# Forward substitution of the RWKV mixer's diagonal blocks: from GpSimd to VectorE, in three stretches for eight

## The chip, the cores and the metric

The kernel runs on one core of one Trainium2 chip. The time is device microseconds of one execution; it is timed several times and the median counts. The engines go by the profile's names: PE is TensorE's matmul, PEld its weight load, DVE is VectorE, ACT is ScalarE, POOL is GpSimd, SP is the engine that only issues DMAs. Each engine works through its own queue in order; engines wait for each other by semaphores.

## The reference

One step of a two-layer network, D = 2048, on 288 tokens: 256 of a prompt and 32 of a running stream. Layer 0 mixes with an mLSTM and an RG-LRU, layer 1 with RWKV-7 (32 heads of 64 channels); each layer ends with a squared-ReLU MLP. All is fp32. The change lies in layer 1's token mixer, whose core is a recurrence over tokens:

```python
def step(S, inp):
    r_t, k_t, v_t, kk_t, a_t, w_t = inp
    sa = jnp.einsum('bhvk,bhk->bhv', S, -kk_t)
    S = S * w_t[:, :, None, :] + sa[..., None] * (kk_t * a_t)[:, :, None, :] + v_t[..., None] * k_t[:, :, None, :]
    return S, jnp.einsum('bhvk,bhk->bhv', S, r_t)
```

The kernel does it in chunks of 64 tokens. Within a chunk the updates form a unit triangular system, so that each head and chunk needs T = (I - M)^-1 of a strictly triangular 64 x 64 matrix M. There are 32 heads and 5 chunks, 160 such matrices.

## The kernel before

All matmuls are three passes in two float32r parts: a weight slab of 128 x 1024 is loaded (`raw`), its high part `whi` is copied by ACT and its low part `wlo` is subtracted on DVE (line 132, shown as L78 since a helper issues it).

The stage that matters comes after the projections of k. Heads go in 16 pairs. Three streams are traced side by side at line 1216, and the framework's list scheduler puts their instructions in order on each engine, by priority and by its own estimate of when each can start; the order is then fixed in the program.

- `front(p)` (line 981), two pairs at a time: elementwise work on DVE and ACT for one pair (`tw`, `L`, `kkn`, `big`), ten small matmuls that give M of the pair (line 1027, shown in traces as `pm<-big`), then `nm`, M masked, on DVE (line 1036). `nm` goes to DRAM as `n` (line 1042) and `big` as well (line 1044).
- `inverse16(q)` (line 1049), two at a time, q = 0 to 7: for the pairs 2q and 2q + 1. The 80 diagonal blocks of 16 x 16 (2 pairs, 2 heads, 5 chunks, 4 blocks each) come back from DRAM as `nb` [80, 16, 16] (line 1055, a DMA issued by POOL), `tb` is loaded with unit matrices, and 15 steps of forward substitution run on the 80 partitions at once, each a product `tmp<-nb,tb` and a sum `tb<-tb,tmp` of (15 - s)(s + 1) elements, 15 to 64. This is called a solve below; it is 30 operations, and 240 in the eight. It runs on `IE`, which is POOL. After each odd s the generator yields, so it is traced in eight stretches. The result goes to DRAM as `t` (line 1070, two DMAs).
- `inverse(p, nm)` (line 1082), run for the two pairs when the solve is through: `tq` comes back from DRAM (line 1089, issued by POOL), DVE transposes it to `xq` (line 1108), PE multiplies it with `nm` (line 1109, in traces `pm<-tq,nm`), DVE masks the product to `zz`, PE multiplies (`pm<-zz,xq`), DVE adds to `t32` and transposes it to `x32`; from there the off-diagonal block (`pm<-t,nm`, `pm<-z,x`) and T of the pair, to DRAM at line 1148.
- Beside them the dense products of v and r (`ps<-hC,whi` and the like), 931 matmuls of 288 columns in this stage.

`nm` has 7 buffers, so that front p waits for the inverse of pair p - 7; `nb` has one buffer, so that the next one is loaded when the solve has read the last one; `whi` and `wlo` have three. The stage that follows, `wkv`, has an order written out by hand; its first matmul transposes `bk` (`pm<-cst,bk`, line 1283). It starts when the last inverse is through.

Of the kernel before, what the change touches and what calls it, by code (L numbers as in the profile page):

```python
# [11 lines left out]
OP = mybir.AluOpType  # L12
# [4 lines left out]
N = NP + NS  # L17
KT = D // 128
KS = 8
# [17 lines left out]
# columns of the constants  # L37
# [4 lines left out]
def stream_step(ctx: ExitStack, tc: tile.TileContext, I, O):  # L42
# [92 lines left out]
    def slab_in(src, pool_, tag, w):  # L135
        """slab, its parts in tiles of another pool"""
        raw = wp.tile([128, KS, 128], F32, name="raw", bufs=3)
        SP.dma_start(raw, src)
        hi, lo = ([pool_.tile([128, N], F32R, name=f"{c}s", tag=tag, bufs=32)[:, :256].rearrange("p (a b) -> p a b", a=2)
                   for _ in range(KS // 2)] for c in "hl")  # L140
        w += [(hi[k // 2][:, k % 2], lo[k // 2][:, k % 2]) for k in range(KS)]
        for j in range(KS // 2):
            r = raw[:, 2 * j:2 * j + 2]
            copy(hi[j], r)
            yield
            tt(lo[j], r, hi[j].bitcast(F32), OP.subtract)
# [25 lines left out]
    def dense(srcs, xs, m=128):  # L172
        """psum[m, N] = W.T @ x; srcs: one DRAM slab for every KS tiles of xs"""
        ps = psum.tile([128, 512], F32, name="ps", bufs=NPS)
        n = len(xs)
        for s, src in enumerate(srcs):
            kt = min(KS, n - s * KS)
            wh, wl = slab(src, kt, m)
            for k in range(kt):
                g = s * KS + k  # L180
                mm3(ps[:m, :N], (wh[:, k, :], wl[:, k, :]), xs[g], g == 0, g == n - 1)
        return ps[:m, :N]

    def load2(pl, src, bufs):
        """slab of two tiles, in space of its own"""
        raw = pl.tile([128, 2, 128], F32, name="raw2", bufs=bufs)
        SP.dma_start(raw, src)
        return raw
# [19 lines left out]
    def dense_g(srcs, xs, m=128, step=4, rest=1):  # L208
        """dense, which lets others on after every step tiles; two at a time"""
        yield from hold()  # L210
        ps = psum.tile([128, 512], F32, name="ps", bufs=NPS)
        n = len(xs)
        for s, src in enumerate(srcs):
            kt = min(KS, n - s * KS)
            wh, wl = slab(src, kt, m)
            for k in range(kt):
                g = s * KS + k
                mm3(ps[:m, :N], (wh[:, k, :], wl[:, k, :]), xs[g], g == 0, g == n - 1)
                if g % step == step - 1:
                    for _ in range(rest):  # L220
                        yield
        free()
        return ps[:m, :N]
# [11 lines left out]
    def run(*streams, n=0):  # L235
        """traces generators side by side, of each stream as many as its width, until all from stream n on are through"""
        rnd[0] = 0
        while any(gens or on for gens, _, on in streams[n:]):
            rnd[0] += 1
            for gens, width, on in streams:  # L240
                while gens and len(on) < width:
                    on.append(gens.pop(0))
                step(on)
# [12 lines left out]
    # squares are taken of d = y - c, where c is the mean of the first CF tiles:  # L256
    # (mean - c)^2 <= (KT / CF - 1) var, so that var = E d^2 - (E d)^2 loses next to nothing
    CF = 2

    class Norm:  # L260
# [7 lines left out]
        def before(self, x, scale=None):  # L268
            """what the next tile is added to, times scale: takes c off already"""
            if len(self.ys) >= CF:  # L270
                if scale:
                    stt(x, x, scale, self.cen, OP.mult, OP.subtract)
                else:
                    tt(x, x, self.cen, OP.subtract)
            elif scale:
                ts(x, x, scale, None, OP.mult, OP.bypass)

        def add(self, y):
            """takes the next tile; the last is left out of the sums"""
            k = len(self.ys)  # L280
            self.ys.append(y)
            if k == 1:
                gadd(self.acc, self.ys[0], y)
            elif 1 < k < CF:
                gadd(self.acc, self.acc, y)
            if k == CF - 1:
                pc = pm()[:, :N]
                mm(pc, ones, self.acc)
                act(self.cen, pc, AF.Copy, scale=1.0 / (128 * CF))
                for j in range(CF):  # L290
                    tt(self.ys[j], self.ys[j], self.cen, OP.subtract)
                    self.sums(j)
            elif k >= CF:
                self.sums(k)
# [14 lines left out]
        def finish(self, gname, bname, out, mid=lambda k: [], subv=(0,)):  # L309
# [22 lines left out]
            with tc.manual_schedule():  # L332
# [5 lines left out]
                # two steps of third order: r <- r (15 - 10 h + 3 h^2) / 8, h = x r^2  # L338
# [34 lines left out]
    class Lead:  # L373
        """the first four matrices after a norm, of two slabs each, three of them at a time"""
# [5 lines left out]
        def ahead(self):  # L380
            """the first slabs"""
            for src, w in list(zip(self.srcs, self.w))[:3]:
                run1(slab_in(src[0], *self.pt, w))

        def mid(self, k):
            """the second slabs, in the course of the norm"""
            i = MID.get(k)
            if i is None:
                return []
            return [slab_in(self.srcs[i][1], *self.pt, self.w[i]) if i == 2 else self.second(i)]  # L390
# [27 lines left out]
    # =================================================================  # L418
    # layer 0
    # =================================================================  # L420
# [6 lines left out]
    # gates of the mLSTM, with the first queries  # L427
# [35 lines left out]
    def log1p(out, z, t1, t2):  # L463
        """log(1 + z) for 0 <= z <= 1, by s = z / (2 + z)"""
# [40 lines left out]
    # RG-LRU constants  # L505
# [57 lines left out]
    def mlstm(h, t):  # L563
# [13 lines left out]
        # attention of the tokens  # L577
# [14 lines left out]
        # numerators and the denominator, which every partition gets  # L592
# [20 lines left out]
        # new state  # L613
# [14 lines left out]
        # norm over the head  # L628
# [41 lines left out]
    def lru(g, xp, yg, wg):  # L670
# [19 lines left out]
        # sqrt(1 - a^2) = (1 + a) sqrt(tanh(u / 2)), a = exp(-u)  # L690
# [12 lines left out]
        # tanh gelu  # L703
# [44 lines left out]
    def mlp(layer, xs, first):  # L748
        """X <- alpha X + mlp(X), xs: X in parts"""
# [23 lines left out]
    # the blocks of 16, zero beside the diagonal  # L773
# [9 lines left out]
    def shift(xx, x, k):  # L783
        """the token before, less the token"""
# [12 lines left out]
    # mixes: 0 r, 1 w, 2 k, 3 v, 4 a, 5 g  # L797
# [29 lines left out]
    # =================================================================  # L827
    # layer 1
    # =================================================================
    # per-channel constants  # L830
# [8 lines left out]
    def head_sums(st, x):  # L839
        """st[96, 6] = the sums over the channels of the two heads, for 3 blocks of tokens"""  # L840
        for j in range(3):
            mm(st[:, 2 * j:2 * j + 2], x[:, 96 * j:96 * j + 96], blk[:, 0:128:64])
# [92 lines left out]
    def over_head(pl, y, bufs):  # L935
        """psum[128, N] = y[96, 6] over the channels of a head"""
# [16 lines left out]
    def prod(out, l, x, start=True, stop=True):  # L953
        """out = l^T x for the two heads, which lie on the halves of the partitions"""
# [18 lines left out]
    IE = G  # L973
# [7 lines left out]
    def front(p):  # L981
# [19 lines left out]
        # decays, summed within the chunks  # L1001
# [22 lines left out]
        # strictly lower M = A B^T, as [s, t]  # L1024
# [24 lines left out]
    def inverse16(q):  # L1049
        """(I - M)^-1 of the 16 x 16 blocks on the diagonal, two pairs of heads"""  # L1050
# [7 lines left out]
        for s in range(15):  # L1058
# [4 lines left out]
               tb[:, s, :n].unsqueeze(1).to_broadcast([80, w, n]), OP.mult, eng=IE)  # L1063
            tt(tb[:, s + 1:, :n], tb[:, s + 1:, :n], tv, OP.add, eng=IE)
            if s % 2:
                yield
# [15 lines left out]
    def inverse(p, nm):  # L1082
        """T = (I - M)^-1 for each chunk of the two heads, to DRAM"""
# [67 lines left out]
    def feed():  # L1151
        """the products beside the heads, tile by tile: queries, then the first half of the output projection with what
        it is added to, to DRAM; slabs are loaded two ahead and split one ahead"""
# [77 lines left out]
    def beside(gens, width, gap, other, rate, size):  # L1231
        """traces gens, as many as width at a time and gap rounds apart, with rate steps of other for each of a round"""
# [22 lines left out]
    def wkv(p):  # L1255
# [21 lines left out]
        def tok(x, out):  # L1277
            """[channel, token] to [token, channel], by head and chunk"""
# [38 lines left out]
        # head h of a stack: its own rows, and the other half of the partitions  # L1317
# [19 lines left out]
        # y, which the chunks add up to; the first one of the prompt clears the bank  # L1337
# [5 lines left out]
        def chunk(c, st, pu, pS, out=None):  # L1343
            """adds to y; the state, at sv[., c], to the next place, or to out"""
# [51 lines left out]
        # norm over the head, bonus, gate  # L1396
# [85 lines left out]
def _pack(np, a):  # L1482
    """lays the inputs out for the chip"""
# [5 lines left out]
    def slabs(w, m=128):  # L1489
        """[K, M] -> [M/m, K/1024, 128, KS, m]"""  # L1490
# [88 lines left out]
```

## Time and profile before

| | us |
|---|---|
| three timed runs | 3352.56, 3355.72, 3361.26 (median 3355.72) |
| span of the profiled execution | 3357.0 |
| PE busy | 3231.9 (96%) |
| DVE busy | 2052.6 (61%) |
| ACT busy | 1545.0 (46%) |
| POOL busy | 570.9 (17%) |

The profile is one execution. In the page's slices each digit is a tenth, so PE is at 9 nearly throughout, and at 8 in four of slices 20 to 25, where the clock row falls too. One slice is 84 us. The stage of the change is some 210 us of that, from about 1890 to 2098 us.

### The profile page before, as it was taken

What the parts mean: (1) busy time and instruction counts of PE and PEld (TensorE: products, weight loads), DVE (VectorE), ACT (ScalarE), POOL (GpSimd) and SP (SyncE); (2) the same over time, 40 slices, a digit from 0 to 9 for tenths busy, and PEclk for the clock granted to TensorE, in tenths of its full rate; (3) what the DMA queues carried; (4) which work ended last, traced back from release to release, by engine and by line L of the source; (5) the groups of instructions that cost most, each with busy time, mean ns of one, the idle gap of its engine ahead of it and who ended that gap; (6) DMA issues with size and microseconds to landing.
All of it is one profiled execution on the core that took longest, in us unless ns stands there. A gap on an engine that the chain in (4) does not pass through costs nothing. (4 is left out here: it accounts for less than half of the span.)

```text
span 3357.0 us, 66280 instructions
## 1 busy us (share of the span) xinstructions
PE 3231.9 (96%) x26763; PEld 3125.1 (93%) x26763; DVE 2052.6 (61%) x3652; ACT 1545.0 (46%) x2816; POOL 570.9 (17%) x891
## 2 busy tenths in 40 slices
PE   9999999999999999999889898999989999999997
PEld 8999999999999999999888887888879999999997
DVE  6777777755644445445589664677775445454455
ACT  4444444433533434344465454666545334343443
POOL 0101110122000000001478365011250000000013
PEclk9999999999999999999899978999989999999998
DMA  5444444455444444444434765434444444444443
GB/s 204 152 151 158 153 153 151 149 177 182 145 168 165 167 166 165 169 165 165 152 125 145 226 202 166 151 130 136 160 150 145 164 169 164 169 164 167 167 164 123
DMA packets 195076, 540.56 MB, mean 161 GB/s; under 512 B 39178, under 2 KB 74250, under 8 KB 194770
## 3 DMA queue, kind: packets, MB, share of 16 engines
q1 hardware_dynamic: 190322, 526.95, 45.7%
q0 software_dynamic: 4448, 9.39, 1.1%
q8 instruction: 210, 3.44, 0.4%
q14 instruction: 96, 0.79, 0.1%
HBM read 500.81 MB, written 35.41 MB: 160 GB/s over the span
## 5 line engine op out<-in xcount | busy, mean ns | idle before, releaser
L78 DVE TENSOR_TENSOR wlo<-raw,whi 128x1024 fp32r<-128x1024 f32 (+1 forms) x1006 | 1088.3, 1089 | 874.9 <-ACT whi L98 870.2
L98 ACT ACTIVATE whi<-raw 128x1024 fp32r<-128x1024 f32 (+1 forms) x1006 | 930.9, 935 | 1191.8 <-PE ps L104 1031.6
L104 PE MATMUL ps<-hB,whi 128*128 128x288 f32 x3696 | 1100.0, 299 | 5.1 <-DVE x L78 2.9
L104 PE MATMUL ps<-lB,whi 128*128 128x288 f32 x3696 | 1092.6, 296 | 5.5 <-DVE lB L78 5.4
L104 PE MATMUL ps<-hB,wlo 128*128 128x288 f32 x3696 | 1091.8, 296 | 3.2 <-DVE wlo L78 3.2
L104 PEld LDWEIGHTS ps<-lB,whi 128*128 128x128 f32 x3696 | 699.6, 189 | 12.8 <-DVE lB L78 8.3
L104 PEld LDWEIGHTS ps<-hB,whi 128*128 128x128 f32 x3696 | 694.5, 188 | 11.0 <-issue 4.5
L104 PEld LDWEIGHTS ps<-hB,wlo 128*128 128x128 f32 x3696 | 698.7, 189 | 5.3 <-DVE wlo L78 4.1
L104 PE MATMUL ps<-hD,whi 128*128 128x288 f32 (+1 forms) x1584 | 476.3, 301 | 0.3 <-ACT whi L98 0.3
L104 PE MATMUL ps<-hD,wlo 128*128 128x288 f32 (+1 forms) x1584 | 469.8, 297 | 6.6 <-DVE wlo L78 6.6
L104 PE MATMUL ps<-lD,whi 128*128 128x288 f32 (+1 forms) x1584 | 468.0, 296 | 1.5 <-DVE lD L78 1.5
L104 PE MATMUL ps<-hC,whi 128*128 128x288 f32 (+1 forms) x1552 | 463.9, 299 | 3.0 <-ACT v L98 3.0
L104 PE MATMUL ps<-hC,wlo 128*128 128x288 f32 (+1 forms) x1552 | 461.6, 298 | 0.0
L104 PE MATMUL ps<-lC,whi 128*128 128x288 f32 (+1 forms) x1552 | 460.8, 297 | 0.0
L104 PEld LDWEIGHTS ps<-hD,wlo 128*128 128x128 f32 (+1 forms) x1584 | 300.3, 190 | 8.1 <-DVE wlo L78 7.8
L104 PEld LDWEIGHTS ps<-hD,whi 128*128 128x128 f32 (+1 forms) x1584 | 299.3, 189 | 4.3 <-issue 1.9
L104 PEld LDWEIGHTS ps<-lD,whi 128*128 128x128 f32 (+1 forms) x1584 | 300.9, 190 | 2.2 <-DVE lD L78 1.7
L104 PEld LDWEIGHTS ps<-hC,whi 128*128 128x128 f32 (+1 forms) x1552 | 295.1, 190 | 4.0 <-ACT v L98 3.7
L104 PEld LDWEIGHTS ps<-lC,whi 128*128 128x128 f32 (+1 forms) x1552 | 296.7, 191 | 0.3
L104 PEld LDWEIGHTS ps<-hC,wlo 128*128 128x128 f32 (+1 forms) x1552 | 295.9, 191 | 0.3
L78 POOL TENSOR_TENSOR acc<-x,x 128x288 f32<-128x288 f32 x8 | 8.6, 1074 | 1484.9 <-DVE x L78 1475.1
L78 DVE TENSOR_TENSOR x<-x,ps 128x288 f32<-128x288 f32 x96 | 43.5, 454 | 96.2 <-PE ps L104 96.2
(347 smaller groups left out, 3391.8 us busy)
## 6 DMA issues: line engine op xcount, KB each, us to landing
raw<-in_w SPq DMA_DIRECT2D x512, 512.0 KB, 3.2
raw<-in_win SPq DMA_DIRECT2D x160, 512.0 KB, 3.2
raw<-in_wout SPq DMA_DIRECT2D x64, 512.0 KB, 3.2
raw<-in_wk SPq DMA_DIRECT2D x32, 512.0 KB, 3.3
raw<-in_wv SPq DMA_DIRECT2D x32, 512.0 KB, 4.0
raw<-in_wr SPq DMA_DIRECT2D x32, 512.0 KB, 3.4
raw<-in_wo SPq DMA_DIRECT2D x32, 512.0 KB, 3.2
big<-big SPq DMA_DIRECT2D x16, 786.5 KB, 5.5
```

What stands on the lines that cost most here:

```text
L78: (eng or V).tensor_tensor(out=out, in0=a, in1=b, op=op)
L98: return A.activation(out, a, f, **kw)
L104: PE.matmul(out, lhsT, rhs, start=start, stop=stop, skip_group_check=True)
```

## The change

`IE` goes, so that the two operations of a step take the default engine of the helper, DVE. The generator yields after steps 4 and 9 alone: three stretches. All else in the file's difference are comments and doc strings; from line 974 on the new file's line numbers are one lower (L1055 becomes L1054). The core of the difference:

```diff
@@ -970,7 +970,6 @@
     NMB = 7
     GAPF = 6
     lastf = [-99]
-    IE = G
     RPC, RPRE, GAP = 4, 4, 11
     WIDTH, RATE, SIZE, EXTRA = 4, 1.8, 4, 0.4
     NG = 1
...
@@ -1060,9 +1059,9 @@
             tmp = t1.tile([80, 64], F32, name="tmp", bufs=2)
             tv = tmp[:, :w * n].rearrange("p (a b) -> p a b", b=n)
             tt(tv, nb[:, s, s + 1:].unsqueeze(2).to_broadcast([80, w, n]),
-               tb[:, s, :n].unsqueeze(1).to_broadcast([80, w, n]), OP.mult, eng=IE)
-            tt(tb[:, s + 1:, :n], tb[:, s + 1:, :n], tv, OP.add, eng=IE)
-            if s % 2:
+               tb[:, s, :n].unsqueeze(1).to_broadcast([80, w, n]), OP.mult)
+            tt(tb[:, s + 1:, :n], tb[:, s + 1:, :n], tv, OP.add)
+            if s in (4, 9):
                 yield
         for i in range(2):
             dst = bass.AP(tensor=S16[q].tensor, offset=S16[q].offset + i * (16 * 32 + 16),
```

The order moves on every engine of the stage. Three places follow; numbers behind a name tell one buffer's use from the next. On DVE, where pair 3 is prepared, the queue before (`big_20982` is pair 3's, `L_21098` belongs to pair 5):

```order
L78 TENSOR_TENSOR wlo2_21147<-raw2_21144,whi2_21146 128x256
L78 TENSOR_TENSOR big_20982<-kkn_21025,big_20982 128x5x63
L1005 SCALAR_TENSOR_TENSOR L_21098<-cst_73,tw_21092 128x320
L84 SCALAR_TENSOR_TENSOR kkn_21025<-ta_20962,kkn_21025 128x288
L1033 MEMSET big_20982 128x32
L1014 MEMSET kkn_21140 128x32
L84 SCALAR_TENSOR_TENSOR big_20982<-kkn_21025,L_20966 128x320
```

and the same place of DVE's queue now, where `big_21005` is pair 3's:

```order
L78 TENSOR_TENSOR wlo2_21201<-raw2_21198,whi2_21200 128x256
L78 TENSOR_TENSOR tmp_20889<-nb_20885,tb_20887 80x15
L78 TENSOR_TENSOR big_21005<-kkn_21036,big_21005 128x5x63
L1004 SCALAR_TENSOR_TENSOR L_21102<-cst_73,tw_21096 128x320
L78 TENSOR_TENSOR tb_20887<-tb_20887,tmp_20889 80x15
L84 SCALAR_TENSOR_TENSOR kkn_21036<-ta_20991,kkn_21036 128x288
L1032 MEMSET big_21005 128x32
L1013 MEMSET kkn_21194 128x32
L78 TENSOR_TENSOR tmp_20892<-nb_20885,tb_20887 80x28
L84 SCALAR_TENSOR_TENSOR big_21005<-kkn_21036,L_20995 128x320
```

The first solve's first operation, which needs `nb`, stands ahead of both `big` rows that the product of pair 3 needs, and two more of its rows stand between them.

On DVE again, from the end of the sixth solve (`tb_22979`) to the transposes of its own result (`xq_23282`, `xq_23305`), the queue now:

```order
L78 TENSOR_TENSOR tb_22979<-tb_22979,tmp_23076 80x15
L78 TENSOR_TENSOR wlo_24038<-raw_24036,whi_24037 128x1024
L78 TENSOR_TENSOR nm_23274<-pm_23243,cst_73 128x320
L1008 MEMSET big_23559 128x32
L1031 COPY big_23559<-big_23559 128x5
L78 TENSOR_TENSOR wlo_24155<-raw_24153,whi_24154 128x1024
L864 MEMSET v_24249 128x32
L1107 STREAM_TRANSPOSE xq_23282<-tq_23213 128x160
L78 TENSOR_TENSOR wlo_24221<-raw_24219,whi_24220 128x1024
L1107 STREAM_TRANSPOSE xq_23305<-tq_23215 128x160
```

Six rows stand between the last operation of the solve and the transpose that needs what the solve's result becomes after two DMAs; before, none of the solve was on this queue.

On PE, the product of pair 4 and the first products of the first inverse, before (`pm_21213` is pair 4's product):

```order
L104 MATMUL pm_21213<-big_21115 64x64 x10
...
L104 MATMUL pm_21240<-tq_21152,nm_20743 32x32 x20
L104 MATMUL pm_21263<-tq_21154,nm_20848 32x32 x20
L942 MATMUL pm_21323<-cst_73,e_21302 128x96 x3
L104 MATMUL ps_21877<-hw_19123,whi2_21808 128x288
```

and now, where `pm_21364` is pair 4's:

```order
L104 MATMUL pm_21127<-tq_21057,nm_20743 32x32 x20
L104 MATMUL pm_21150<-tq_21059,nm_20848 32x32 x20
L942 MATMUL pm_21180<-cst_73,e_21123 128x96 x3
L104 MATMUL pm_21206<-zz_21184,xq_21125 32x32 x20
L104 MATMUL pm_21227<-zz_21186,xq_21148 32x32 x20
L104 MATMUL pm_21319<-t32_21276,nm_20743 32x32 x10
L104 MATMUL pm_21330<-t32_21280,nm_20848 32x32 x10
L104 MATMUL pm_21364<-big_21119 64x64 x10
```

The product of pair 4 has gone behind the first inverse's products, and no dense product stands between them. POOL's queue keeps its DMA issues (`nb`, `t`, `tq`) and loses the 240 operations.

## Rows read from the trace of the kernel before

**Rows 1.** The page: busy us by engine, and PE's clock in 40 slices.

```profile
PE 3231.9 (96%) x26763; PEld 3125.1 (93%) x26763; DVE 2052.6 (61%) x3652; ACT 1545.0 (46%) x2816; POOL 570.9 (17%) x891
...
POOL 0101110122000000001478365011250000000013
PEclk9999999999999999999899978999989999999998
```

**Rows 2.** Busy time by stretch: length, us of each engine (instructions), clock, DMA share, GB/s.

```profile
1892.90:2097.00 204.10, 174.28 (x2969) 160.74 (x2967) 119.60 (x317) 104.68 (x247) 130.53 (x284) 0.85 0.63 191
1250.00:1450.00 200.00, 200.00 (x1515) 200.00 (x1514) 97.72 (x111) 78.70 (x95) 0.00 (x0) 1.00 0.47 166
```

**Rows 3.** Waits, 1892.9 to 2097: total us, times, longest.

```profile
DVE xq L1108 <- DMA tq<-t: 28.2, 12, 7.2
...
DVE wlo L78 <- ACT whi L98: 24.3, 16, 3.4
PE pm L104 <- DMA tq<-t: 19.5, 8, 6.9
POOL tmp L78 <- DMA nb<-n: 18.3, 5, 6.7
```

**Rows 4.** Timeline of POOL: start us, duration us; first and last solve.

```profile
1897.62 0.24 POOL L78 TENSOR_TENSOR tmp<-nb,tb 80x15 f32<-80x15 f32 x1 [6.67 <-DMA nb<-n]
...
1912.68 0.22 POOL L78 TENSOR_TENSOR tb<-tb,tmp 80x15 f32<-80x15 f32 x1
...
2067.34 0.20 POOL L78 TENSOR_TENSOR tmp<-nb,tb 80x15 f32<-80x15 f32 x1 [3.79 <-DMA nb<-n]
...
2080.26 0.28 POOL L78 TENSOR_TENSOR tb<-tb,tmp 80x15 f32<-80x15 f32 x1
```

**Rows 5.** Timeline of DVE around the first and the last solve.

```profile
1881.87 0.49 DVE L78 TENSOR_TENSOR nm<-pm,cst 128x320 f32<-128x320 f32 x1
...
1892.52 0.42 DVE L78 TENSOR_TENSOR wlo<-raw,whi 128x256 fp32r<-128x256 f32 x1
...
1922.28 0.34 DVE L1108 STREAM_TRANSPOSE xq<-tq 128x160 f32<-128x160 f32 x1 [7.19 <-DMA tq<-t]
...
2054.52 0.48 DVE L78 TENSOR_TENSOR nm<-pm,cst 128x320 f32<-128x320 f32 x1
...
2088.52 0.35 DVE L1108 STREAM_TRANSPOSE xq<-tq 128x160 f32<-128x160 f32 x1 [6.74 <-DMA tq<-t]
```

**Rows 6.** Busy time of the instructions on tmp (all 240) in the stretch.

```profile
1892.90:2097.00 204.10, 92.90 (x240) 0.85 0.63 191
```

**Rows 7.** Timeline of DVE, ahead of the stage: small operations.

```profile
1853.14 0.15 DVE L81 TENSOR_SCALAR knorm<-pm 96x6 f32<-96x6 f32 x1
...
1853.57 0.25 DVE L78 TENSOR_TENSOR krt<-kinv 96x96 f32<-96x96 f32 x1
1853.86 0.25 DVE L84 SCALAR_TENSOR_TENSOR krt<-krt,knorm 96x96 f32<-96x96 f32 x1
```

**Rows 8.** Groups by form, DVE, 1892.9 to 2097: busy us, mean ns | idle before.

```profile
L78 DVE TENSOR_TENSOR wlo<-raw,whi 128x1024 fp32r<-128x1024 f32 x27 | 33.1, 1226 | 17.8 <-ACT whi L98 17.6
...
L78 DVE TENSOR_TENSOR big<-kkn,big 128x315 f32<-128x315 f32 x13 | 6.5, 503 | 0.2
...
L78 DVE TENSOR_TENSOR t<-tq,pm 128x160 f32<-128x160 f32 x16 | 4.8, 299 | 6.5 <-PE pm L104 6.5
```

**Rows 9.** Timeline of PE: first tq product, and the wkv stage's first.

```profile
1922.39 0.76 PE L104 MATMUL pm<-tq,nm 32*32 32x32 f32 x40 [6.93 <-DMA tq<-t]
...
2098.46 0.90 PE L1283 MATMUL pm<-cst,bk 128*128 128x128 f32 x3
```

## The prediction

> **What bounds the kernel now.** I read the page first. PE is busy 96% of the span, and its clock is at 9 or more in all but five of 40 slices, lowest in the 24th and 25th (7 and 8) [rows 1]. Outside that dip only less PE work would help, and the change takes none away. POOL is at 6 and 5 in the same two slices [rows 1]: the substitution lies in the dip. The next view was the busy time by stretch. From 1892.9 us (the last VectorE instruction ahead of the place where the first moved one now stands) to 2097.0 (VectorE's last for the inverses) PE is busy 174.3 of 204.1 us at a granted clock of 0.85, POOL 130.5, VectorE 119.6; in a stretch of the MLP PE has 200.0 of 200.0 at 1.00 [rows 2]. So the stage has 30 us of open PE idleness and about as much again hidden in the lower clock, and it is set by waits.
>
> The view of waits names them: PE waits 19.5 us for tq, VectorE 28.2 us for the same tq and 24.3 us for whi, POOL 18.3 us for nb [rows 3]. They lie on one chain, which each of the eight substitutions ("solves") goes through: nm on VectorE, to DRAM and back as nb, the solve, to DRAM and back as tq, then xq on VectorE and the products on PE. For the first solve the timeline gives nm ending at 1881.87 + 0.49 = 1882.36 and its first operation starting at 1897.62: 15.3 us; the solve ends at 1912.90, 15.3 us later; xq starts at 1922.28, 9.4 us later. For the last: nm ends at 2055.00, the solve starts at 2067.34 (12.3), ends at 2080.54 (13.2), xq starts at 2088.52 (8.0) [rows 4, 5]. So the solve is some 14 of 34 to 40 us, and the DRAM trips, which stay, are 20 to 25.
>
> **The change, part by part.** The 240 operations leave POOL, where they are 92.9 us of busy time, 387 ns each [rows 6]. POOL keeps its DMA issues. That frees an engine which is ahead of nobody else in this stretch; what counts is the solve's latency and what VectorE's queue does.
>
> *Cost on VectorE.* No operation of 15 to 64 elements by 80 partitions is there before. The nearest: 96x6 takes 0.15 us, 96x96 0.25 us, and a dependent one starts 0.29 after the one ahead of it, a gap of 0.04 [rows 7]; 128x160 takes 299 ns [rows 8]. The mean solve operation has 45 elements: a line between 0.15 at 6 and 0.25 at 96 gives 0.19 to 0.20 us. I take 0.20, since it lies between two near rows; the ends are 0.15 (36 us) and 0.30 (72 us). Sum: 240 x 0.20 = 48 us, and a solve alone takes 30 x 0.23 = 7 us. [...]
>
> *Is it hidden?* VectorE is idle 204.1 - 119.6 = 84.5 us of the stretch [rows 2], so by the sum alone 48 us fit. But its queue is in order and the new order puts the solves where they wait. Three things in the order count.
>
> First, at a solve's head. tmp<-nb now stands in front of the big<-kkn rows of pair 3, whose product PE comes to at once. In the old timeline VectorE reaches that place at 1892.52 + 0.42 = 1892.9, and nb lands for 1897.6 [rows 4, 5]: 4.7 us of wait, with the pair's elementwise work, its nm and the next weight split queued behind it. Before, only POOL stood there. For solves 2 and 4 some 6 us of work stand between nm and the solve's first row against 12.3 of trip; part of the rest is taken by waits for PE, and I count 4 us each; 1.5 and 2.5 for solves 6 and 7. For solves 1, 3 and 5 this wait falls inside the next one. Together 16.7 us.
>
> Second, between a solve's last row and its own xq. Counted in the new order, at the durations of the trace (a 128x1024 split 1.23 us, a 128x315 product 0.50 [rows 8], less what neighbours overlap, a solve operation 0.20), the work there is 3.4, 6.5, 3.0, 5.8, 2.5, 2.9, 4.9 and 0 us for the eight. The trip is 9.4 us, 8.0 for the last [rows 4, 5]. VectorE must stand for 6.0 + 2.9 + 6.4 + 3.6 + 6.9 + 6.5 + 4.5 + 8.0 = 44.8 us, where it waits 28.2 now [rows 3]. It can't fill these gaps, because the work that did now stands inside the solves.
>
> Third, inside the solves. Between first and last row of the eight there are 28, 6, 24, 24, 32, 39, 26 and 9 rows of other work, of 11, 2, 10, 7, 11, 13, 12 and 3 us. So the solve's latency isn't 7 us but 6 plus these: 17, 8, 16, 13, 17, 19, 18 and 9 us, a mean of 15, against POOL's 13 to 15. The latency that the move should save goes back to interleaving in six of eight.
>
> *PE's side.* PE now reaches the first tq product after 152 dense products behind the product of pair 1, not 203, and the product of pair 4 stands behind it, not ahead. PE was already 6.9 us too early there [rows 9], so this wait grows. Over the stage the same 931 dense products run; PE's 174 busy us, part of them at the lower clock, fit under VectorE's sum, so I don't add PE.
>
> *The sum.* VectorE's queue from 1892.9 on: work 119.6 + 48 = 167.6; waits for nb 16.7; waits for tq 44.8; dependence gaps of 0.04 in unbroken runs, some 70 of them, 3. Together 232.1 against 204.1: +28 us. The later wkv stage has the same order and moves as a whole. Weight-split waits (24.3 us, [rows 3]) I set at nothing: they come when VectorE is ahead of PE and the slab buffers are full, and VectorE is late now. If all stay, +24 more. The profiled span is 3357.0 us, 1.3 above the median of the three timed runs (3355.72), so the sum gives 3385.0 by the span and 3383.7 by the median: **3384 us**.
>
> **The rivals.**
> *A, faster: the solve's latency decides.* POOL goes through a solve, its four result issues and the nb issue in turn; first rows of the first and last solve are (2067.34 - 1897.62) / 7 = 24.2 us apart per solve [rows 4]. If POOL's lap is the pace, replacing a 14 us solve by 7 to 9 us shortens it by 5 to 7, eight times; PE's idleness of 30 us caps that: about 3357 - 30 = 3327 us. For it: PE's longest waits are for tq [rows 3]. Against it: six of the eight solves are interleaved, and the trips stay. [...]
> *B, no change.* VectorE's 84.5 idle us take the 48, the nb and tq waits merge with the waits for PE that are there now (24.3 and the rest), and the solves' spread makes up. Then 3351 to 3364, middle 3357.
> *C, clearly worse.* As forecast, and longer PE waits keep the clock at the lower level for longer. In the stretch it is 0.85 [rows 2]; at 0.78 the 174 us of PE work would grow by some 9% or 16 us, and with operations at 0.30 us another 24. PE then joins VectorE in the bound: about 3384 + 40 = 3424 us.
>
> **How the numbers follow.** Forecast (3366 to 3410) 0.62; A 0.12; B 0.16; C 0.10. The forecast's own range is from its terms: operations at 0.15 us take 12 off and the first-row waits count 17, half of which could merge, so about 3364; operations at 0.30 add 24, some of the split waits a few more, so 3410. The range to hold 8 in 10 takes in B from its middle and the lower part of C: 3352 to 3415. About 0.3%, 10 us, is what a measurement of this kernel tells from no change. Faster by more: A, 0.12. Within: B, 0.16 less what of it lies outside, and nothing of the forecast, 0.15. Slower: 0.73.
>
> **What would show it.** The step on cost: tmp and tb on VectorE at 0.17 to 0.23 us. The step on the head: VectorE waits for nb, first at tmp of the first solve, and the product of pair 3 waits for big. The step on xq: VectorE's wait for tq grows from 28 to some 45 us. The step on interleaving: first to last row of most solves 13 to 19 us, of the second and last 7 to 10. The sum: the first product of the wkv stage at about 2126 instead of 2098.5 us [rows 9], and everything before 1890 and behind unchanged. I am wrong if the stage ends earlier than now, if VectorE's idle time shrinks by the full 48 us with the end in place, or if the time is lost outside the stretch.

## The result and the profile after

The changed kernel takes 3383.9 us (median of 4 runs, 3379.5 to 3387.6) against 3358.2 for the kernel before on the same chip: a ratio of 1.0085, 95% interval 1.0073 to 1.0097. So it is slower, by some 26 us as the difference of these medians and some 28 us by the ratio. 3384 was forecast. The profiled execution has a span of 3385.8 us, 28.8 longer than that of before.

The page after, busy us by engine and the slices of POOL and of PE's clock, against [rows 1]:

```profile
PE 3233.8 (96%) x26763; PEld 3127.3 (92%) x26763; DVE 2084.0 (62%) x3892; ACT 1546.1 (46%) x2816; POOL 477.5 (14%) x651
...
POOL 0101010113000000002576111101250000000013
PEclk9999999999999999999899878999999999999998
```

The 240 operations have moved, and the dip of the clock is one slice longer. The timeline of PE after, against [rows 9] (start, duration, then the wait ahead of it):

```profile
1922.82 0.76 PE L104 MATMUL pm<-tq,nm 32*32 32x32 f32 x40 [11.39 <-DMA tq<-t]
...
2127.29 0.90 PE L1282 MATMUL pm<-cst,bk 128*128 128x128 f32 x3
```

The wkv stage begins 2127.29 - 2098.46 = 28.8 us later, and what follows takes 1258.5 us in both (3357.0 - 2098.46, 3385.8 - 2127.29). Up to 1890 us PE runs 13521 products in both. So the whole loss lies in the stage of the inverses. Its busy time after, up to the first wkv product:

```profile
1892.90:2127.29 234.39, 178.33 (x2985) 164.43 (x2983) 153.71 (x556) 106.27 (x251) 37.32 (x44) 0.79 0.56 166
```

And the waits of the same stretch, against [rows 3]:

```profile
PE pm L104 <- DMA tq<-t: 33.5, 8, 11.4
...
DVE xq L1107 <- DMA tq<-t: 28.2, 9, 8.8
...
DVE wlo L78 <- ACT whi L98: 13.9, 15, 2.6
...
DVE tmp L78 <- DMA nb<-n: 8.8, 5, 3.6
```

Two things stand here against the forecast: VectorE's wait for tq is 28.2 us as before, not 45; and PE's, which the forecast didn't add, went from 19.5 to 33.5.

**The ledger that closes.** Over such a stretch PE's busy time and PE's waits, all rows of the view of waits for that engine added up, give the length to within 1 us in every kernel run here. Before: 175.3 + 30.1 = 205.4 of 205.6. After: 178.3 + 55.7 = 234.0 of 234.4. So the 28.8 us are 3.1 of busy time and 25.6 of waits of PE, 14.0 of these for tq, 7.0 for ScalarE, 1.9 for VectorE. Such a sum comes near on other engines too (VectorE after: 153.7 + 73.5 = 227.2 of 234.4), so that it says where PE's time goes and not what made PE wait. The table has this for all kernels, always from 1892.9 us to the first wkv product. "Rounds" are the turns that other work gets between the start of a solve and its inverses: the yields inside the solve and the empty ones behind it. The kernel before has 7 + 5 = 12; the change takes five of the seven away and leaves 2 + 5 = 7.

| kernel | solve on | rounds | ratio to before, 95% interval | median us | first wkv product | PE busy | PE waits | for tq | for VectorE | for ScalarE |
|---|---|---|---|---|---|---|---|---|---|---|
| before | POOL | 12 | 1 | 3358.2 | 2098.46 | 175.3 | 30.1 | 19.5 | 4.6 | 5.0 |
| after | VectorE | 7 | 1.0085 (1.0073, 1.0097) | 3383.9 | 2127.29 | 178.3 | 55.7 | 33.5 | 6.5 | 12.0 |
| e1 | POOL | 7 | 1.0083 (1.0061, 1.0105) | 3384.0 | 2126.26 | 177.1 | 56.0 | 43.3 | 1.5 | 8.2 |
| e2 | VectorE | 12 | 1.0055 (1.0038, 1.0073) | 3372.5 | 2109.36 | 176.0 | 40.3 | 18.9 | 13.1 | 6.6 |
| e3 | POOL, and 240 operations on VectorE | 12 | 1.0059 (1.0036, 1.0081) | 3375.9 | 2115.25 | 171.6 | 50.4 | 38.2 | 7.7 | 2.3 |
| e4 | VectorE, wlo on POOL | 7 | 1.0123 (1.0096, 1.0149) | 3398.4 | 2132.55 | 184.3 | 55.5 | 12.9 | 27.7 | 6.6 |
| e5 | VectorE | 10 | 1.0108 (1.0093, 1.0123) | 3391.5 | 2130.79 | 180.3 | 56.6 | 24.6 | 13.8 | 14.5 |
| e6 | VectorE | 15 | 1.0050 (1.0034, 1.0067) | 3373.2 | 2116.98 | 173.6 | 50.0 | 21.2 | 14.9 | 11.1 |
| e7 | VectorE | 20 | 1.0043 (1.0028, 1.0058) | 3370.5 | 2108.96 | 168.2 | 47.2 | 26.5 | 5.9 | 10.0 |
| e8 | POOL | 15 | 0.9995 (0.9986, 1.0004) | 3353.3 | 2092.82 | 167.8 | 32.1 | 21.0 | 3.4 | 3.3 |
| e9 | VectorE, half the steps | 12 | 1.0000 (0.9990, 1.0010) | 3356.3 | 2098.01 | 178.7 | 26.2 | 8.5 | 10.2 | 6.5 |
| e10 | POOL, half the steps | 12 | 0.9993 (0.9984, 1.0003) | 3353.5 | 2094.82 | 172.7 | 29.1 | 9.8 | 15.3 | 3.7 |
| e11 | VectorE, ta on POOL | 12 | 1.0066 (1.0046, 1.0085) | 3375.5 | 2124.43 | 182.7 | 49.6 | 13.8 | 11.5 | 21.3 |
| e12 | POOL, the last on VectorE | 15 | 0.9993 (0.9982, 1.0004) | 3352.3 | 2089.75 | 166.8 | 29.9 | 17.6 | 3.0 | 5.6 |

The medians of before beside e1 to e12 were 3355.0, 3354.9 and 3354.1 us. The profiled execution of one kernel can lie some 10 us off its median (e11: 3385.9 against 3375.5, e2: 3365.8 against 3372.5), so ratios are for the time and the ledger is for where it goes.

### The profile page after: what moved, and what is told of

Same layout as the page of the kernel before. It is cut to its first block, busy times and chain, and to the rows that moved or that the text cites. A ratio compares the mean times of both kernels' runs of the same rounds, so it can differ in the third digit from the quotient of the medians.

```text
span 3385.8 us, 66294 instructions
## 1 busy us (share of the span) xinstructions
PE 3233.8 (96%) x26763; PEld 3127.3 (92%) x26763; DVE 2084.0 (62%) x3892; ACT 1546.1 (46%) x2816; POOL 477.5 (14%) x651
## 4 chain that ended last, share of the span: by engine, by line
PE 37%; DVE 5%; DMA 3%; POOL 2%; issue 2%; ACT 1%; SPq 0%; ACTq 0%; DVEq 0%; POOLq 0%
PE ps L104 31%; PE pm L104 4%; DVE wlo L78 1%; PE py L104 1%; DVE x L78 1%; DMA tq<-t 1%; DMA t<-tb 1%; POOL xx L78 1%; DMA xres<-xp 1%; PE pm L1282 1%; DVE mx L84 1%; DMA nb<-n 0%; DMA n<-nm 0%; ACT whi L98 0%; DVE tb L78 0%
```

## The experiments

The theories, as the expectations name them. Q, the forecast: VectorE's in-order queue holds the solves and their waits. S: the new stretches reorder every engine, whatever runs the solve. W: the plain work added to VectorE. R: S made precise, the number of rounds counts. L: the latency of a solve counts. T: any other order than that of before costs some 20 us.

**e1, three stretches, POOL.**

```diff
-            if s % 2:
+            if s in (4, 9):
                 yield
```

> The substitution stays on POOL but is handed over in three stretches (after steps 4 and 9) as in the changed kernel, not in eight: the half of the change that is only about stretches. Theory Q (the forecast: the loss comes from VectorE's in-order queue, which holds the solves and their waits): POOL still has nothing else to do, so 3350 to 3365 us, VectorE's wait for tq near 28 us. Rival S (the new places of the stretches reorder all engines, and that order is what costs): 3375 to 3390 us, with the stage's end near 2125 us as in the changed kernel.

3384.0 us, as S said. Without one operation moved to VectorE, the loss is the whole of the change's. The waits of PE in e1, from 1892.9 to 2126.26 us, all of them:

```profile
PE pm L104 <- DMA tq<-t: 43.3, 10, 11.1
PE ps L104 <- ACT v L98: 6.1, 4, 2.8
PE pm L104 <- issue: 3.0, 3, 1.8
PE pm L104 <- DVE t L78: 1.2, 2, 0.7
PE pm L104 <- ACT z L98: 1.0, 2, 0.7
PE ps L104 <- ACT ta L98: 0.8, 1, 0.8
PE pm L104 <- DVE big L84: 0.3, 1, 0.3
PE ps L104 <- ACT tw L98: 0.3, 1, 0.3
```

The first tq wait is 11.10 us in e1 and 11.39 in the changed kernel, 6.93 before [rows 9]: PE comes to that product behind 152 dense products in both, not 203. Over the eight solves the order has a mean of 162 dense products between the last product that a solve needs and the first that needs its result; e1 has 136, the changed kernel 147. So the missing rounds leave PE less dense work to cover the way through a solve and its transfers.

That this cover is what costs is not shown, because the chain of work that ended last, as the profile infers it, is hardly on PE in e1. Its shares of the stretch, for e1 and then for the changed kernel (the view cuts long lines):

```profile
by line: POOL tb L78 21.7%; POOL tmp L78 18.7%; DMA nb<-n 15.6%; DMA t<-tb 14.8%; issue 13.8%; DMA n<-nm 4.7%; DMA tq<-t 3.4%; POOL t L1070 2.7%; POOL tq L1089 2.0%; PE pm L104 1.1%; ACT tts L98 0.9%; SPq L1042 0.6%; ACT z L98 0.4%; SPq L12
by line: PE ps L104 16.5%; PE pm L104 10.7%; issue 9.9%; DMA tq<-t 9.8%; DMA t<-tb 9.4%; DMA nb<-n 6.2%; DVE tb L78 4.2%; DVE tmp L78 4.0%; DVE wlo L78 3.6%; DMA n<-nm 2.5%; DVE kkn L84 2.4%; PE pm L942 1.8%; ACT tts L98 1.8%; DMA raw<-in_l
```

In e1 the solves on POOL have 40% of it, the transfers of n, nb, t and tq 38%, PE 1%; in the changed kernel PE has 27% and the solves on VectorE 8%. From one solve's first row to the next's it is 28.7 us on the mean in e1 and 24.2 before [rows 4], while a solve itself takes 13.8 and 13.9. What grew are waits between two solves. The three in the next lines were 18.3 [rows 3], 6.7 and 5.9 us before and are in e1:

```profile
POOL tmp L78 <- DMA nb<-n: 30.0, 7, 5.7
POOL tq L1089 <- DMA t<-tb: 24.3, 6, 6.0
...
POOL nb L1055 <- DMA n<-nm: 18.0, 3, 9.9
```

Two turns of e1's chain show where they come from, the way from the end of the fourth solve to the fifth and from the sixth to the seventh:

```profile
1990.21 0.91 POOL t L1070
1991.12 5.77 DMA t<-tb
...
1997.52 1.04 POOL tq L1089 x2
...
1999.27 5.38 DMA nb<-n
...
2053.09 3.22 DMA t<-tb
...
2056.45 0.33 SPq L1057
...
2057.35 0.59 SPq L1042
...
2057.99 4.46 DMA n<-nm
...
2063.11 5.30 DMA nb<-n
```

In the first, POOL stands at its issue of tq until t has landed, and the issue of the next nb stands behind it in POOL's queue. In the second, SP stands at the load of the unit matrices into `tb` (line 1057) until the sixth solve's result has left that buffer, and the store of the next nm (line 1042), which was ready at 2051.89 us, stands behind it. The missing rounds reorder every queue at once; no run separates PE's order from that of the two queues that issue these transfers.

That the rounds count and not the stretches is read from the instruction order alone: with ten empty rounds behind three stretches (12 in all), POOL's version has on every engine the order of the kernel before, and VectorE's that of e2, instruction for instruction.

**e2, eight stretches, VectorE.**

```diff
-            if s in (4, 9):
+            if s % 2:
                 yield
```

> The substitution on VectorE, in eight stretches as before: the other half of the change alone. Q: 3375 to 3400 us, since VectorE's queue holds the solves all the same; more rows of other work fall into the solves (46, 6, 35, 40, 24, 37, 22, 11 in the order against 28, 6, 24, 24, 32, 39, 26, 9), so rather the upper half. S: within 10 us of the kernel before, 3347 to 3367.

3372.5 us, just under Q's range and above S's: neither half of the change is free, yet 29 and 17 us alone make 26 together. In e2 PE's wait for tq is that of before (18.9); what grew are waits for results of VectorE, 4.6 to 13.1 us:

```profile
PE pm L104 <- DMA tq<-t: 18.9, 9, 7.2
...
PE pm L104 <- DVE t L78: 5.2, 5, 1.6
PE pm L104 <- DVE big L84: 3.5, 3, 2.4
PE pm L104 <- DVE zz L78: 3.5, 4, 1.4
```

Why they don't add is seen in two rows of e1, VectorE's wait for tq and the busy time by engine, beside those of the changed kernel above. In e1 VectorE waits 54.4 us for tq and is busy 119.18; in the changed kernel 28.2 and 153.71. So by these totals 26 of the 34.5 us of new work lie in a wait that the missing rounds had opened; row by row this was not shown.

```profile
DVE xq L1108 <- DMA tq<-t: 54.4, 11, 9.4
```

```profile
1892.90:2126.26 233.36, 177.11 (x2983) 163.84 (x2982) 119.18 (x311) 105.50 (x251) 129.59 (x284) 0.81 0.56 165
```

**e3, POOL's solve and an equal load on VectorE.**

```diff
+    xt = t1.tile([80, 64], F32, name="xt", bufs=1)
...
-            tmp = t1.tile([80, 64], F32, name="tmp", bufs=2)
+            tmp = t1.tile([80, 64], F32, name="tmp", bufs=1)
...
             tt(tb[:, s + 1:, :n], tb[:, s + 1:, :n], tv, OP.add, eng=IE)
+            ev = xt[:, :w * n].rearrange("p (a b) -> p a b", b=n)
+            tt(ev, ident[:80, :w].unsqueeze(2).to_broadcast([80, w, n]),
+               ident[:80, :n].unsqueeze(1).to_broadcast([80, w, n]), OP.mult)
+            tt(ev, ev, ident[:80, :w].unsqueeze(2).to_broadcast([80, w, n]), OP.add)
```

> The kernel before, with the substitution on POOL in eight stretches, and beside each of its operations an operation of the same size on VectorE that works on constants only: it waits for no transfer, and nobody waits for its result. So VectorE has the 240 operations (some 47 us) without the waits and without the shorter latency. Theory W (the work itself: VectorE's rows lie in the lap from the fronts to the solve, and 6 us more per lap delay nm): 3372 to 3390 us, most of the loss. Theory Q (the waits in the queue make most of the loss; 86 us of idle time take the work): 3352 to 3368 us.

3375.9 us, in W's range. PE's wait for tq doubles to 38.2, that for VectorE goes from 4.6 to 7.7. But e3 doesn't measure work alone: PE's order changed too (a mean of 138 dense products per solve, not 162), `tmp` has one buffer where it had two, POOL's solves got longer (15.7 us on the mean, not 13.9), and 39 of the 240 added operations ran ahead of 1892.9 us.

**e4, the changed kernel with the weight splits of the stage on POOL.**

```diff
-            wh, wl = slab(src, kt, m)
+            wh, wl = slab(src, kt, m, SE[0])
...
+    SE[0] = G
     run(stream([front(p) for p in range(PAIRS)], 2), ...
```

> The changed kernel, and in this stage the low halves of the weight splits (wlo, 27 of 128x1024 with 33 us of VectorE's time) are taken by POOL, which the change left idle. W: the work of VectorE falls back to about that of the kernel before, so most of the 28 us comes back: 3352 to 3368 us. Q: the waits at nb and tq stay where they are in the queue and the time stays at 3372 to 3390 us. A slower split on POOL could add waits of PE for the weights to either; that would show in the waits of PE and POOL's busy time per wlo.

3398.4 us, slower than either theory said. VectorE's busy time rose to 170.4 us though 33 us of splits had left it. The timeline of both engines shows why:

```profile
1900.92 0.22 DVE L78 TENSOR_TENSOR tmp<-nb,tb 80x60 f32<-80x60 f32 x1
1901.14 2.40 POOL L78 TENSOR_TENSOR wlo<-raw,whi 128x1024 fp32r<-128x1024 f32 x1 [5.24 <-ACT whi L98]
1901.17 2.45 DVE L78 TENSOR_TENSOR tb<-tb,tmp 80x60 f32<-80x60 f32 x1
1903.66 0.22 DVE L78 TENSOR_TENSOR tmp<-nb,tb 80x63 f32<-80x63 f32 x1
```

The operation of VectorE that starts at 1901.17 beside POOL's split of 2.40 us lasts 2.45 us, and its neighbours last 0.22; in e4 ten operations of solves start during a split, and nine of them last at least to its end. e4 can't judge W.

**e5 to e8, the number of rounds.** e5, e6 and e7 put 8, 13 and 18 empty rounds behind VectorE's solve in three stretches (10, 15, 20 in all), e8 puts 8 behind POOL's in eight (15):

```diff
-        for _ in range(5):
+        for _ in range(8):
             yield
         on = [inverse(2 * q, NM[2 * q]), inverse(2 * q + 1, NM[2 * q + 1])]
```

> The changed kernel with 8 empty rounds between a solve and its inverses instead of 5, so a pair of heads passes 10 rounds of the streams there (2 in the stretches, 8 empty), where the changed kernel has 7 and the kernel before 12. Theory R (what the three stretches cost is the rounds that they take out: other work is traced in those rounds, and it stands ahead of the tq products on PE and VectorE): between the changed kernel's 3384 and the 3372.5 of VectorE with 12 rounds, 3371 to 3381 us, PE's wait for tq between 33 and 19 us. Rival W (VectorE's added work is the loss, rounds don't matter on VectorE): 3378 to 3390 us. Rival T (the kernel before stands at a point chosen for its order, and any other order costs some 20 us, without direction): 3365 to 3395 us, with no relation to the waits for tq.

> The changed kernel with 13 empty rounds, 15 in all. R: PE's and VectorE's waits for tq shrink further (below 15 us each in the stage) and the time is that of 12 rounds or less, 3355 to 3373 us. W: 3372 to 3390. T: above 3375 us.

> The changed kernel with 18 empty rounds, 20 in all: the far end. R: the waits for tq are nearly gone, but the chain of each pair takes more rounds and the last inverses come later; 3360 to 3385 us. W: 3372 to 3390. T: above 3375 us.

> The kernel before (substitution on POOL in eight stretches) with 8 empty rounds instead of 5, 15 in all. R: POOL had 43 us of PE's waits for tq at 7 rounds and 19.5 at 12; at 15 they fall below 15 us and the time is 3345 to 3358 us. T: slower than before, above 3362 us. W says nothing of it: within 10 us of 3355.

e5, 3391.5 us, misses R's and W's ranges: PE's wait for tq falls as R said (24.6), but its waits for ScalarE and VectorE grow to 14.5 and 13.8, so the time isn't a smooth function of the rounds; T's range holds it. e6, 3373.2, is at the edge of R's range, in W's, and without the fall in the tq waits that R named; e7, 3370.5, fits R's range for the time, again without that fall (26.5), and lies below W's. e8 refutes T, which had it above 3362: with 15 rounds POOL's version is as fast as with 12. R's time holds there, but not the tq waits below 15 us that it named (21.0). At 15 rounds VectorE costs 3373.2 - 3353.3 = 20 us more than POOL, at 12 rounds 17, at 7 rounds nothing.

**e9 and e10, half of the steps**, on VectorE and on POOL, 12 rounds:

```diff
-        for s in range(15):
+        for s in range(0, 15, 2):
...
-            if s % 2:
+            if s < 14:
                 yield
```

> VectorE with 12 rounds as in the run of the engine alone (3372.5 us against 3355), but only steps 0, 2, ..., 14 of the 15 are computed, with a round after each but the last; the inverse is not the right one. About half of the 240 operations and of their 48 us go. Theory W (with 12 rounds or more, what VectorE costs is the work in its queue): half of the 17.5 us comes back, 3358 to 3368 us. Rival L (the latency of the solve decides): the solve gets shorter by a third or more on every lap, 3335 to 3357 us. Rival Q (waits at the head of the solves and at xq, which stay whole): 3368 to 3380 us.

> The kernel before with the same half of the steps left out on POOL (12 rounds; the inverse is not the right one): POOL's solve takes about 7 us instead of 14, VectorE's work is that of the kernel before. L: 3320 to 3345 us, since each of eight laps loses up to 6 us. W: the latency of the solve has cover in 12 rounds of other work; 3345 to 3358 us, the last solve alone giving 6 us, which nothing covers.

e10 misses L's range and fits W's: POOL's solves take 7.2 us on the mean of eight instead of 13.9, and the time is 0.9993 of before. PE's wait for tq halves, and its wait for big, which the fronts deliver, takes the place:

```profile
PE pm L104 <- DVE big L84: 12.8, 4, 5.5
PE pm L104 <- DMA tq<-t: 9.8, 5, 2.9
```

So a solve half as long brought no gain on POOL. That its length has no price doesn't follow, because the shorter solve gave PE another order as well: 133 dense products per solve on the mean, not 162. e1 has 136, with solves of 13.8 us and 7 rounds, and takes 3384.0 us.

e9 falls in L's range: without half of the operations all of the 17 us are back. Its solves take 11.6 us on the mean where e2's take 18.2, and PE's order moved too (145 dense products per solve, in e2 165), so that e9 doesn't tell the work from the length of a solve.

**e11, VectorE with 12 rounds, the four operations from ta on POOL.**

```diff
-        tt(kh[:, :N], ta, L[:, :N], OP.mult)
+        tt(kh[:, :N], ta, L[:, :N], OP.mult, eng=G)
```

(and in the same way the two operations on ta ahead of it and the product with rk behind it)

> VectorE with 12 rounds, and four operations for each pair that are off the way to nm (the two of ta, kh and the product with rk, 64 in all with some 22 us of VectorE's time) on the idle POOL. W: 22 of the 48 us are off the queue again: 3357 to 3367 us. Q: the waits stay: 3368 to 3380 us. POOL's issues of nb and tq stand behind these operations now; if that delays them, the time goes up and POOL's waits ahead of nb and tq show it.

3375.5 us: W's range is missed, Q's is met. POOL takes 1.0 to 1.15 us for each of these operations, VectorE's tmp now has a longest of 0.83 us instead of 0.22, and xq starts 12.1 us behind a solve's end on the mean (e2: 10.7), with POOL's issues of t and tq now in the queue of these operations. The busy time of e2 and of e11, in which the third figure after the length is VectorE's:

```profile
1892.90:2109.36 216.46, 176.04 (x2975) 160.59 (x2973) 152.74 (x556) 105.00 (x251) 37.41 (x44) 0.82 0.59 175
1892.90:2124.43 231.53, 182.74 (x3003) 168.10 (x3003) 149.85 (x510) 107.40 (x257) 93.36 (x98) 0.82 0.58 173
```

It fell by 2.9 us, where some 22 were to leave (a part of them ahead of this stretch), and the operations of the solves took 56.9 us in all instead of 46.9. Like e4, e11 hardly took time off VectorE, and can't judge W.

**e12, POOL with 15 rounds and the last solve on VectorE.**

```diff
-               ..., OP.mult, eng=IE)
+               ..., OP.mult, eng=V if q == PAIRS // 2 - 1 else G)
```

> POOL with 15 rounds (3353.3 us), and only the last of the eight solves on VectorE, where no other work is left beside it: the version to which the runs point. The last solve takes 8.6 us on VectorE against 13.2 on POOL. W: that 4.6 us is all gain: 3346 to 3352 us. L would give the same here. If the stage's end isn't set by the last solve: 3350 to 3357 us as without.

3352.3 us: faster than the changed kernel, and not to be told from the kernel before (interval 0.9982 to 1.0004); W's 3346 to 3352 us are missed by a little, and the range for a stage whose end the last solve doesn't set holds. VectorE's rows of the last solve in e12:

```profile
2062.07 0.17 DVE L78 TENSOR_TENSOR tmp<-nb,tb 80x15 f32<-80x15 f32 x1 [1.46 <-issue]
...
2073.02 0.17 DVE L78 TENSOR_TENSOR tb<-tb,tmp 80x15 f32<-80x15 f32 x1
2081.16 0.35 DVE L1108 STREAM_TRANSPOSE xq<-tq 128x160 f32<-128x160 f32 x1 [7.96 <-DMA tq<-t]
```

Ten rows of other work stand inside, so it takes 11.1 us, not the 8.6 that I counted on, against 11.6 on POOL in e8.

## Why the forecast was right, and where its reason was not

*The place* was right: the stage alone, with the first wkv product forecast at 2126 and measured at 2127.29.

*Cost on VectorE*: right for the operation. Its rows after, least, median and longest ns:

```profile
L78 DVE TENSOR_TENSOR tmp<-nb,tb x120: 128/196/221, 1896.0 to 2108.2; 80x15 f32<-80x15 f32 x16, 80x28 f32<-80x28 f32 x16, 80x39 f32<-80x39 f32 x16, 80x48 f32<-80x48 f32 x16
L78 DVE TENSOR_TENSOR tb<-tb,tmp x120: 138/198/223, 1897.3 to 2108.4; 80x15 f32<-80x15 f32 x16, 80x28 f32<-80x28 f32 x16, 80x39 f32<-80x39 f32 x16, 80x48 f32<-80x48 f32 x16
```

But VectorE's busy time grew by 34.1 us [rows 2], not by 48. The 240 operations alone are busy for 46.95 us after; yet rows overlap their neighbours in the trace (`big` starts at 1896.14 us, where the `tmp` ahead of it starts at 1896.05 and lasts 0.17), and the durations of VectorE's rows add up to some 26 us more than its busy time in the stretch, where before it was some 15.

*Interleaving*: right. The latencies are 18.6, 9.1, 15.5, 16.5, 15.3, 21.4, 18.6 and 8.6 us, a mean of 15.4 where 15 was forecast. What it costs is not shown (e9, e10).

*Head and xq*: too large. The waits for nb are 8.8 us where 16.7 were forecast, those for tq 28.2 where 44.8 were. The first two solves, by VectorE's timeline after, against [rows 4, 5]:

```profile
1896.05 0.17 DVE L78 TENSOR_TENSOR tmp<-nb,tb 80x15 f32<-80x15 f32 x1 [3.56 <-DMA nb<-n]
...
1914.43 0.17 DVE L78 TENSOR_TENSOR tb<-tb,tmp 80x15 f32<-80x15 f32 x1
1917.81 0.17 DVE L78 TENSOR_TENSOR tmp<-nb,tb 80x15 f32<-80x15 f32 x1 [3.21 <-DMA nb<-n]
...
1922.71 0.35 DVE L1107 STREAM_TRANSPOSE xq<-tq 128x160 f32<-128x160 f32 x1 [0.87 <-DMA tq<-t]
```

The wait at the first head is near the 4.7 that were forecast. At xq VectorE waits 0.87 us and not 6.0, because the second solve's head, with a wait of its own, stands ahead of it.

*PE's side*: The forecast saw that PE reaches the first tq product after 152 dense products instead of 203, called the wait to grow, and added nothing, because it summed VectorE's queue. PE's wait for tq grew by 14.0 us and all of its waits by 25.6.

*The step that failed* is the path. The forecast laid the loss to VectorE's queue and called POOL an engine "which is ahead of nobody else in this stretch"; it read the three stretches only as a part of the new order, and no rival priced them alone. e1 has no solve in VectorE's queue and loses as much (1.0083 against 1.0085), and POOL's solves are 40% of the chain that ends its stage. With 7 rounds the move to VectorE adds nothing to be seen; with 12 it costs 17 us.

*The sum*: that 232.1 us came near to 234.4 is luck. The terms named give 153.7 of busy time, 8.8 for nb and 28.2 for tq, 191 us; the other 44 are waits that were set at nothing (13.9 for whi, 6.6 for big, 5.2 for v and smaller ones) and gaps. The same terms for the kernel before, 119.6 of work and 28.2 for tq, give 147.8 of its 204.1 us: the forecast set a part of the new queue against the whole of the old one, and terms that were too large made up for those left out.

*The rivals.* A (the solve's length decides, so faster) did not come: the solves got no shorter here (15.4 us on the mean against 13.9), and in e10, where they are half as long, the time is that of before. The operation itself is faster on VectorE, with a median of 196 ns for `tmp` after against 284 on POOL before, a factor of 1.4, and the kernel is slower all the same. B (VectorE's idle time hides the work) holds at 7 rounds, where e1 and the changed kernel differ by 0.1 us, and not at 12. C: with PE's waits at 55.7 us instead of 30.1 the granted clock did fall, from 0.85 to 0.79, but PE's busy time grew by 3.1 us, not by 16.

*What stays open*: which of the reordered queues makes the loss of the missing rounds, PE's with less cover or POOL's and SP's with the issues. Why VectorE costs 17 to 20 us at 12 rounds and more is open as well. e2's ledger names waits of PE for VectorE's results; but its solves also take 18.2 us on the mean against 13.9 before, because 6 to 46 rows of other work stand in each. e9 gives all of it back with both the work and the length cut, and e4 and e11 hardly took time off VectorE. No run holds PE's order fixed and changes the load alone. Why e5 is the slowest of VectorE's versions that keep all other work in place is open too.

## What to carry to other kernels

Do a sum of a stretch for the kernel before first: if its terms don't give the measured length there, they can't be trusted for the change. A sum that closes says where one engine's time goes; the chain that ended last says on which queue a loss may arise. Where generators are traced round by round, a yield that is taken out is an edit of its own: it moves everybody else's work, and a run with the yields alone is the first to make. Two losses need not add: here 29 and 17 us made 26.

## What the runs showed of the hardware

In the traces of before and of e4 an operation of a solve beside a weight split of the other engine lasted longer than alone. In e4 POOL's 128x1024 split takes a median of 2.39 us (a mean of 1.22 on VectorE in the changed kernel) and an operation of a solve on VectorE that starts during it lasts up to 2.45 us, where the median of all 240 is 0.20; two that met two splits in a row lasted 4.63 and 5.87. One operation, at 1965.29 us, kept its 0.20. Before, it went the other way: POOL's tmp has a median of 284 ns, and the 17 longest of its solves' 240 operations, 1100 to 1378 ns, all lie beside VectorE's splits of 1226 ns [rows 8]; the 88 beside which VectorE has no row last 200 to 320. What holds them up is not shown. So work moved from VectorE to POOL was not off VectorE's hands here: in e4, which moves 33 us of splits, VectorE's busy time is 170.4 us against 153.7 in the changed kernel, and in e11, which moves some 22 us, it is 149.9 against 152.7 in e2.

The granted clock is a mean over a stretch with waits in it: in e7 it is 0.82 and PE is busy for 168.2 us, before it was 0.85 and 175.3. By itself it didn't price the work here.
